# Sums of weight blocks on VectorE in place of accumulating DMAs, in the gate pairs and the heads' projection of a hybrid decoder block

## The chip, the core and the metric

The kernel runs on one core of a Trainium2 chip. A core has TensorE (PE, matmuls, with its weight loads shown as PEld), ScalarE (ACT), VectorE (DVE), GpSimd (POOL) and SyncE (SP), each with a queue of instructions that it takes in order, and 16 DMA engines that all issuing engines share. The metric is the device time of one execution in microseconds (us).

## The reference

One decoder layer in float32 on 512 tokens and a model width of 1024. What matters here is that nearly all of its work is matrix products with weights from HBM:

```python
hn = rmsnorm(x, g_mix[l])
proj = jnp.einsum('bsd,de->bse', hn, w_in[l])
(xa, ba, ca, za, q, k, v, o, zb, ig, fg, ga, gb) = jnp.split(proj, SPLIT_POINTS, axis=-1)
...
hb = mlstm_chunkwise(q, k, v, ig, fg)            # 4 heads, DK 256, DV 512
yb = jax.nn.sigmoid(o) * hb * jax.nn.silu(zb)
yb = jnp.einsum('bsv,vd->bsd', yb, w_b_out[l])   # the heads' projection
merged = jax.nn.sigmoid(ga) * ya + jax.nn.sigmoid(gb) * yb
x = x + jnp.einsum('bsd,de->bse', merged, w_o[l])
```

ga and gb are the gates, 1024 columns each of `w_in`; `ig` and `fg` are eight columns, one input and one forget gate for each head.

## The kernel before

**Products.** Every float32 operand is split into a high part (rounded to the type that the matmul takes, `whi`, by ACT, L152) and a low rest (`wlo`, by DVE, L153); a product is three matmuls, hi x hi, hi x lo, lo x hi (`mm3`, L205 to L207). Weights come in chunks of 512 rows by 512 columns (1 MB, tile `wraw`, a ring of four) by DMA from SP's queue (L135). Each chunk is split in two halves of 256 rows.

**Strassen pairs.** Most of the projections are done with seven block products in place of eight. `pair` lists, for two by two blocks b11, b21, b12, b22 of the weights, the seven right operands in the order of use: b11, b21, b11 + b12, b22, and so on. The sums are made in place: b11 is the first operand, b12 is then added to it and it is the third, b22 is added and it is the fifth, b21 is added and it is the seventh; b22 is also added to b12 for the sixth. So a pair has four sums of two halves each. A sum is made either by an accumulating DMA on POOL's queue (L159), which reads the block from HBM once more and adds it to the tile in SBUF, or by DVE (L157), which adds one tile to another and thus needs both in SBUF. `third` says which engine makes the sum b12 + b22; the other three are DMAs. Each entry of `operands` is (chunk, sums after its split); `last_use` says when a tile of the ring is free, and `load_free` then loads the next chunk.

**Order of the work.** The order on PE, ACT, DVE and POOL is written out by hand (`manual_schedule`); SP's is set by the scheduler. PE's matmuls of a product come in two parts (banks) of 12 matmuls. After each part `step` calls `tick` (L188): it starts the generators of the part before, splits one half of a chunk (`split_half`, L148, followed by its sums), and advances the generators in `active` by one yield. So a yield is one tick later.

**The stages.** First x is normalised and transposed; then the blocks q, k of heads 1 and 0. Beside these run two generators: `gate_rows` (L650 to L699, the logarithm L663, scans of the input and forget gates on DVE, ending with the row of L689, which PE transposes into `ptc` at L694 and L696) and `left` (L609), which makes the sums of hn for all later Strassen products: four DVE sums (L612, L613, L615, L616) and four splits into `hs` (ACT L620, DVE L622 and L625). Then for each head: a pair for v and o, and, around heads 0 and 2, a pair for z of two heads and one for a gate (gb at head 0, ga at head 2; `sink_gate`). After head 1 there is a pair for q, k of heads 2 and 3. While a gate pair runs, `turn` transposes the finished head (copies `yc`, L745) and writes it to HBM (`yt_d`, 1 MB, POOL's queue, L753), and `recut` loads q and k of the next odd head (`qk_raw`, SP's queue, L765) and cuts them in high and low (L212, L213). `yc` and `qk_raw` use the same place in SBUF, so the loads wait for the write. Then come the convolution, its projection, the heads' projection (a Strassen product with two groups of rows, so that its 14 operands are chunks of `w_b_out`; its left operands are `units`, split one by one by `left_high`, L966 to L978, in the generator `left_heads`, from sums in `hsf`, tiles `yhs`), `w_o`, and the gated embedding.

## Time and profile before

| what | value |
|---|---|
| median of 3 runs | 878.53 us (873.56 to 879.10) |
| the profiled execution | 876.83 us, its span 875.1 us |
| PE busy | 851.2 us, 97% |
| DVE, ACT, POOL busy | 612.3, 482.7, 233.5 us |
| accumulating DMAs on `w_in`, `w_b_out` | 122 and 16, 1.4 and 1.6 us to issue each |
| POOL's DMA queue | 78.1 MB, 46.8% of the time of the 16 DMA engines |
| SP's DMA queue | 91.8 MB, 32.0% |

A group or row of the profile names line, engine, operation and output<-input by the names of the program. Times on a timeline are from the start of the span. "Idle before" is how long the engine stood before the instruction, with the one that released it. PE's matmuls overlap: one of 512 columns is shown as 0.39 us long but the next can start before it ends, so the time that a stop costs is read from start to start.

### The profile page before, as it was taken

What the parts mean: (1) busy time and instruction counts of PE and PEld (TensorE: products, weight loads), DVE (VectorE), ACT (ScalarE), POOL (GpSimd) and SP (SyncE); (2) the same over time, 40 slices, a digit from 0 to 9 for tenths busy, and PEclk for the clock granted to TensorE, in tenths of its full rate; (3) what the DMA queues carried; (4) which work ended last, traced back from release to release, by engine and by line L of the source; (5) the groups of instructions that cost most, each with busy time, mean ns of one, the idle gap of its engine ahead of it and who ended that gap; (6) DMA issues with size and microseconds to landing.
All of it is one profiled execution on the core that took longest, in us unless ns stands there. A gap on an engine that the chain in (4) does not pass through costs nothing.

```text
span 875.1 us, 12147 instructions
## 1 busy us (share of the span) xinstructions
PE 851.2 (97%) x4651; PEld 737.8 (84%) x4651; DVE 612.3 (70%) x798; ACT 482.7 (55%) x700; POOL 233.5 (27%) x230
## 2 busy tenths in 40 slices
PE   7999999999999999999899999999999999999996
PEld 6887888877889988888678999999998888788885
DVE  4777657845677667687558678898986777874465
ACT  6557665656666475566576455555553256534342
POOL 4102213312232424222023324234310214130031
PEclk9999999999999999999999999999999999999998
DMA  8847779999995997789999699899998588994002
GB/s 279 276 145 146 142 169 200 230 277 266 232 216 127 255 243 171 158 228 238 272 234 247 116 213 188 196 157 200 181 302 319 107 194 209 265 332 166 1 1 96
DMA packets 105402, 174.92 MB, mean 200 GB/s; under 512 B 6592, under 2 KB 47616, under 8 KB 104064
## 3 DMA queue, kind: packets, MB, share of 16 engines
q0 software_dynamic: 42256, 78.13, 46.8%
q1 hardware_dynamic: 60784, 91.83, 32.0%
q10 hardware_dynamic: 2304, 4.20, 1.4%
q8 instruction: 36, 0.59, 0.3%
q14 instruction: 22, 0.18, 0.1%
HBM read 157.35 MB, written 16.78 MB: 199 GB/s over the span
## 4 chain that ended last, share of the span: by engine, by line
PE 78%; DMA 6%; DVE 3%; ACT 3%; issue 1%; ACTq 0%; SPq 0%; POOL 0%; POOLq 0%; DVEq 0%
PE mm L206 24%; PE mm L207 24%; PE mm L205 24%; DMA wraw<-in_w_in 2%; DMA wraw<-in_w_b_out 2%; ACT whi L152 1%; DVE wlo L153 1%; DMA qk_raw<-qk_d 1%; PE pv L205 1%; PE pv L206 1%; PE pv L207 1%; PE pty L750 1%; PE sc L207 1%; PE sc L206 1%; PE sc L205 1%
## 5 line engine op out<-in xcount | busy, mean ns | idle before, releaser
L153 DVE TENSOR_TENSOR wlo<-wraw,whi 128x1024 fp32r<-128x1024 f32 x240 | 298.2, 1246 | 142.2 <-ACT whi L152 141.1
L152 ACT ACTIVATE whi<-wraw 128x1024 fp32r<-128x1024 f32 x242 | 253.2, 1054 | 115.4 <-PE mm L207 43.7
L159 POOL DMA_DIRECT2D wraw<-in_w_in x122 | 149.2, 1411 | 341.4 <-DVE wlo L153 240.0
L321 ACT ACTIVATE s<-mm 128x512 f32<-128x512 f32 x84 | 50.1, 597 | 96.1 <-PE mm L207 94.2
L205 PE MATMUL mm<-whi,hs 128*128 128x512 f32 x256 | 100.5, 392 | 1.2 <-ACT whi L152 1.2
L206 PE MATMUL mm<-wlo,hs 128*128 128x512 f32 x256 | 100.6, 393 | 0.8 <-DVE wlo L153 0.8
L207 PE MATMUL mm<-whi,hs 128*128 128x512 f32 x256 | 100.3, 392 | 0.0
L205 PE MATMUL mm<-hn_hi,whi 128*128 128x256 f32 (+1 forms) x304 | 93.9, 309 | 0.0
L207 PE MATMUL mm<-hn_hi,wlo 128*128 128x256 f32 (+1 forms) x304 | 93.7, 308 | 0.2 <-POOL wlo L153 0.2
L206 PE MATMUL mm<-hn_lo,whi 128*128 128x256 f32 (+1 forms) x304 | 93.6, 308 | 0.0
L205 PE MATMUL mm<-hs,whi 128*128 128x256 f32 x320 | 90.9, 284 | 0.0
L206 PE MATMUL mm<-hs,whi 128*128 128x256 f32 x320 | 90.5, 283 | 0.0
L207 PE MATMUL mm<-hs,wlo 128*128 128x256 f32 x320 | 90.5, 283 | 0.0
L205 PE MATMUL mm<-whi,hn_hi 128*128 128x512 f32 x192 | 75.6, 394 | 3.2 <-ACT s L321 3.2
L206 PE MATMUL mm<-wlo,hn_hi 128*128 128x512 f32 x192 | 75.2, 392 | 2.1 <-DVE wlo L153 2.1
L207 PE MATMUL mm<-whi,hn_lo 128*128 128x512 f32 x192 | 74.7, 389 | 0.0
L206 PEld LDWEIGHTS mm<-hs,whi 128*128 128x128 f32 x320 | 61.4, 192 | 0.0
L205 PEld LDWEIGHTS mm<-hs,whi 128*128 128x128 f32 x320 | 61.4, 192 | 0.0
L207 PEld LDWEIGHTS mm<-hs,wlo 128*128 128x128 f32 x320 | 61.4, 192 | 0.0
L207 PEld LDWEIGHTS mm<-hn_hi,wlo 128*128 128x128 f32 x304 | 58.5, 192 | 3.3 <-POOL wlo L153 0.6
L206 PEld LDWEIGHTS mm<-hn_lo,whi 128*128 128x128 f32 x304 | 58.4, 192 | 2.5
L205 PEld LDWEIGHTS mm<-hn_hi,whi 128*128 128x128 f32 x304 | 58.4, 192 | 2.5
(278 smaller groups left out, 1657.7 us busy)
## 6 DMA issues: line engine op xcount, KB each, us to landing
wraw<-in_w_in SPq DMA_DIRECT2D x32, 1024.0 KB, 7.2
wraw<-in_w_in POOLq DMA_DIRECT2D x62, 512.0 KB, 8.2
wraw<-in_w_in SPq DMA_DIRECT2D x48, 512.0 KB, 5.3
wraw<-in_w_in POOLq DMA_DIRECT2D x60, 256.0 KB, 5.8
wraw<-in_w_b_out SPq DMA_DIRECT2D x8, 1024.0 KB, 7.0
wraw<-in_w_b_out POOLq DMA_DIRECT2D x16, 512.0 KB, 7.1
yt_d<-yc POOLq DMA_DIRECT2D x4, 1024.0 KB, 7.0
wraw<-in_w_a_out SPq DMA_DIRECT2D x4, 1024.0 KB, 5.4
```

The source lines that it names most:

```text
L152: act.activation(hi, t, AF.Copy)
L153: (e_lo or dve).tensor_tensor(lo, t, hi.bitcast(F32), ALU.subtract)
L159: nc.gpsimd.dma_start(raws[to][:, ks, cs], src[:, ks, :], accum_op=ALU.add)
L205: pe.matmul(ps, lhsT=a[0], rhs=b[0], start=first, stop=False, **kw)
L206: pe.matmul(ps, lhsT=a[0], rhs=b[1], start=False, stop=False, **kw)
L207: pe.matmul(ps, lhsT=a[1], rhs=b[0], start=False, stop=last, **kw)
L321: act.activation(to[i], src, AF.Copy, scale=scale)
L750: pe.transpose(pts[v][:, t * P:(t + 1) * P], y[:, t, v * P:(v + 1) * P], ident)
```

## The change

`pair` gets a number in place of an engine: with `on_dve` 1 the sum b12 + b22 is DVE's, as `third` did; with 2 the sums b11 + b12 and b11 + b22 are DVE's too, and the chunks are loaded in the order b11, b12, b21, b22. Both gate pairs get 2 (the first had none, the second one). In the heads' projection the sum b12 + b22 of both groups becomes DVE's; that of group 1 comes after operand 9 and not 8. Chunk b12 of group 0 (`spare`) is loaded not into the ring but into the place of the two `yhs` tiles, once `left_high` has split the last unit made from them (k == 5); `load_free` does not count it in the ring. `left` starts with a yield and is appended beside `gate_rows`, ahead of the second half of the first q, k block. `recut` waits one yield more between its loads and its first cut. The same sums and products are made as before.

```diff
@@ -81,13 +81,18 @@
         for k0 in halves:
             operands.append((chunk(view, k0, pieces), []))
 
-    def pair(view, p1, p2, third=None):
-
-
-        b11, b21, b12, b22 = (chunk(view, k, p) for p, k in ((p1, 0), (p1, HC), (p2, 0), (p2, HC)))
-        t3 = [(b12, b22, third)]
-        operands.extend([(b11, [(b11, b12, None)]), (b21, [] if third else t3), (b11, [(b11, b22, None)]),
-                         (b22, t3 if third else []), (b11, [(b11, b21, None)]), (b12, []), (b11, [])])
+    def pair(view, p1, p2, on_dve=0):
+
+
+
+        where = ((p1, 0), (p2, 0), (p1, HC), (p2, HC)) if on_dve == 2 else ((p1, 0), (p1, HC), (p2, 0), (p2, HC))
+        b11, b21, b12, b22 = (chunk(view, k, p) for p, k in where)
+        if on_dve == 2:
+            b12, b21 = b21, b12
+        e2, e3 = (dve if on_dve >= n else None for n in (2, 1))
+        t3 = [(b12, b22, e3)]
+        operands.extend([(b11, [(b11, b12, e2)]), (b21, [] if e3 else t3), (b11, [(b11, b22, e2)]),
+                         (b22, t3 if e3 else []), (b11, [(b11, b21, None)]), (b12, []), (b11, [])])
 
 
     chunks.append([(w_ple_v[:, k:k + 1, n * CW:(n + 1) * CW], slice(2 * n + k, 2 * n + k + 1), slice(0, CW))
@@ -100,21 +105,23 @@
         pair(w_in_v, [(V + h * DV, DV)], [(O + h * DV, DV)])
         if h % 2 == 0:
             pair(w_in_v, [(ZB + h * DV, DV)], [(ZB + (h + 1) * DV, DV)])
-            pair(w_in_v, [((GB, GA)[h // 2], CW)], [((GB, GA)[h // 2] + CW, CW)], dve if h else None)
+            pair(w_in_v, [((GB, GA)[h // 2], CW)], [((GB, GA)[h // 2] + CW, CW)], 2)
         elif h == 1:
-            pair(w_in_v, *([(Q + i * DK, DK), (K + i * DK, DK)] for i in (2, 3)), dve)
+            pair(w_in_v, *([(Q + i * DK, DK), (K + i * DK, DK)] for i in (2, 3)), 1)
     for c in range(0, KT * P, 2 * P):
-        pair(w_in_v, *([(o + c, 2 * P) for o in os] for os in ((XA, CA), (BA, ZA))), dve)
+        pair(w_in_v, *([(o + c, 2 * P) for o in os] for os in ((XA, CA), (BA, ZA))), 1)
     for n in range(2):
         block(w_a_v, [(n * CW, CW)])
 
     b11, b21, b22, b12 = ([chunk(w_b_v, (2 * g + r) * HC, [(n * CW, CW)]) for g in range(2)]
                           for r, n in ((0, 0), (1, 0), (1, 1), (0, 1)))
-    adds = {1: [(b11, b12, 1)], 5: [(b11, b22, 1)], 7: [(b12, b22, 0)], 8: [(b11, b21, 0), (b12, b22, 1)], 9: [(b11, b21, 1)]}
-    adds.update({0: [(b11, b12, 0)], 4: [(b11, b22, 0)]})
+    spare = {b12[0]: None}
+    adds = {0: [(b11, b12, 0, None)], 1: [(b11, b12, 1, None)], 4: [(b11, b22, 0, None)], 5: [(b11, b22, 1, None)],
+            7: [(b12, b22, 0, dve)], 8: [(b11, b21, 0, None)], 9: [(b12, b22, 1, dve), (b11, b21, 1, None)]}
     for j, u in enumerate((b11, b21, b11, b22, b11, b12, b11)):
         for g in range(2):
-            operands.append((u[g], [(to[i], c[i], None) for to, c, i in adds.get(2 * j + g, ())]))
+            operands.append((u[g], [(to[i], c[i], e) for to, c, i, e in adds.get(2 * j + g, ())]))
+    place_b12 = b12[0]
     for view in (w_o_v, w_pg_v):
         for n in range(2):
             block(view, [(n * CW, CW)], (HC, 0) if view is w_o_v and n == 0 else (0, HC))
@@ -122,22 +129,27 @@
     last_use = {}
     for i, (r, add) in enumerate(operands):
         last_use[r] = i
-        for to, _, _ in add:
+        for to, c, eng in add:
             last_use[to] = i
+            if eng is not None:
+                last_use[c] = i
     state = {"raw": 0, "split": 0, "use": 0}
     raws, splits, pieces, active, fresh = {}, {}, deque(), [], []
 
     def load_raw(between=None):
         i = state["raw"]
         state["raw"] += 1
-        raws[i] = wraw.tile([P, HC, CW], F32, name=f"wraw{i}", tag="wraw")
+        raws[i] = spare[i] if i in spare else wraw.tile([P, HC, CW], F32, name=f"wraw{i}", tag="wraw")
         for src, ks, cs in chunks[i]:
             nc.sync.dma_start(raws[i][:, ks, cs], src)
             if between:
                 between = between()
 
     def load_free():
-        while state["raw"] < len(chunks) and len(raws) < NRAW:
+        while state["raw"] < len(chunks):
+            i = state["raw"]
+            if (spare[i] is None) if i in spare else (sum(c not in spare for c in raws) >= NRAW):
+                break
             load_raw()
 
     def split_tiles(i, h):
@@ -609,6 +621,7 @@
         a11, a12 = (hnf[:, c * HC:(c + 1) * HC, :H2] for c in range(2))
         a21, a22 = (hnf[:, c * HC:(c + 1) * HC, H2:] for c in range(2))
         hsf = [sp.tile([P, HC, H2], F32, name=f"hsf{i}", tag=f"hsf{i}", align_bytes=256) for i in range(2)]
+        yield
         dve.tensor_tensor(hsf[0], a22, a21, ALU.subtract)
         dve.tensor_tensor(hsf[1], hsf[0], a11, ALU.add)
         yield
@@ -708,6 +721,7 @@
         pe.matmul(psg, lhsT=wg[:, k, :], rhs=hn_hi[:, k, :], start=k == 0, stop=False)
         pe.matmul(psg, lhsT=wg[:, k, :], rhs=hn_lo[:, k, :], start=False, stop=k == KT - 1)
     active.append(gate_rows())
+    active.append(left())
     for m in range(4):
         for kt in range(HC):
             mm3(pss[m], [u[kt][:, m * P:(m + 1) * P] for u in w], [u[:, HC + kt, :] for u in hn],
@@ -722,7 +736,6 @@
             yield
         return sink
 
-    active.append(left())
     qk_0 = []
     block_fm(lambda m, ps: keep_qk(m, ps, qk_0))
     drain()
@@ -763,6 +776,7 @@
         raw = hp.tile([P, 2, 4, S], F32, name="qk_raw", tag="vv", align_bytes=256)[:, 0]
         for m in range(4):
             nc.sync.dma_start(raw[:, m, :], qk_d[h][:, m, :])
+        yield
         yield
         yield
         qk.extend(qk_tile())
@@ -963,7 +977,8 @@
     yf = [wbp.tile([P, 2, HC, H2], F32, name=f"yf{h}") for h in range(NH)]
     for h in (0, 2, 1, 3):
         nc.gpsimd.dma_start(yf[h], yt_d[h])
-    hsf = [wbp.tile([P, HC, H2], F32, name=f"yhs{g}") for g in range(2)]
+    hsf = wbp.tile([P, 2, HC, H2], F32, name="yhs", tag="yhs", align_bytes=256)
+    hsf = [hsf[:, g] for g in range(2)]
     units = {}
 
     def left_high(k):
@@ -1004,6 +1019,9 @@
             low = left_high(k)
             yield
             low()
+            if k == 5:
+                spare[place_b12] = wbp.tile([P, HC, CW], F32, name="wraws", tag="yhs", align_bytes=256)
+                load_free()
             if k == 3:
                 yield
                 dve.tensor_tensor(yf[3][:, 0], yf[2][:, 0], yf[3][:, 0], ALU.subtract)
```

DVE's queue where the z projection of head 0 ends and its gate pair begins: `wlo` of chunk `wraw_1192` is the low half of b11, that of `wraw_1280` (before) or `wraw_1360` (after) of b21, which is the second operand; `c`, `sz` and `gty` belong to z. Before:

```order
L153 TENSOR_TENSOR wlo_1429<-wraw_1192,whi_1428 128x1024
L918 TENSOR_TENSOR c<-sz,c 128x512
L922 TENSOR_TENSOR sz<-sz,mm 128x512
L923 TENSOR_TENSOR gty<-gty,sz 128x512
L153 TENSOR_TENSOR wlo_1454<-wraw_1192,whi_1453 128x1024
L918 TENSOR_TENSOR c<-sz,c 128x512
L922 TENSOR_TENSOR sz<-sz,mm 128x512
L923 TENSOR_TENSOR gty<-gty,sz 128x512
L153 TENSOR_TENSOR wlo_1480<-wraw_1280,whi_1479 128x1024
L900 SCALAR_TENSOR_TENSOR gty<-gty,cols 128x512
L153 TENSOR_TENSOR wlo_1501<-wraw_1280,whi_1500 128x1024
L900 SCALAR_TENSOR_TENSOR gty<-gty,cols 128x512
```

After:

```order
L165 TENSOR_TENSOR wlo_1429<-wraw_1192,whi_1428 128x1024
L169 TENSOR_TENSOR wraw_1192<-wraw_1192,wraw_1280 128x1024
L932 TENSOR_TENSOR c<-sz,c 128x512
L936 TENSOR_TENSOR sz<-sz,mm 128x512
L937 TENSOR_TENSOR gty<-gty,sz 128x512
L165 TENSOR_TENSOR wlo_1454<-wraw_1192,whi_1453 128x1024
L169 TENSOR_TENSOR wraw_1192<-wraw_1192,wraw_1280 128x1024
L932 TENSOR_TENSOR c<-sz,c 128x512
L936 TENSOR_TENSOR sz<-sz,mm 128x512
L937 TENSOR_TENSOR gty<-gty,sz 128x512
L165 TENSOR_TENSOR wlo_1480<-wraw_1360,whi_1479 128x1024
L914 SCALAR_TENSOR_TENSOR gty<-gty,cols 128x512
```

Two sums stand between the low halves of the first operand and those of the second; in the queue behind this, two sums more follow the third operand and two the fourth.

DVE's queue ahead of the transposes into `ptc`; `rows` and `carry` are the scans of the gates, `hs` the low halves of `left`, L689 (now L702) the row that PE needs. Before:

```order
L684 SCALAR_TENSOR_TENSOR rows<-rows 4x128
L682 TENSOR_TENSOR carry<-rows 4x1
L684 SCALAR_TENSOR_TENSOR rows<-rows,carry 4x128
L622 SCALAR_TENSOR_TENSOR hs_116<-hsf_561,hs_115 128x1024
L153 TENSOR_TENSOR wlo_645<-wraw_333,whi_644 128x1024
L682 TENSOR_TENSOR carry<-rows 4x1
L684 SCALAR_TENSOR_TENSOR rows<-rows,carry 4x128
L682 TENSOR_TENSOR carry<-rows 4x1
L684 SCALAR_TENSOR_TENSOR rows<-rows,carry 4x128
L622 SCALAR_TENSOR_TENSOR hs_118<-hnf,hs_117 128x1024
L153 TENSOR_TENSOR wlo_670<-wraw_333,whi_669 128x1024
L689 SCALAR_TENSOR_TENSOR rows<-rows 4x512
```

After:

```order
L635 SCALAR_TENSOR_TENSOR hs_114<-hsf_484,hs_113 128x1024
L697 SCALAR_TENSOR_TENSOR rows<-rows 4x128
L695 TENSOR_TENSOR carry<-rows 4x1
L697 SCALAR_TENSOR_TENSOR rows<-rows,carry 4x128
L638 SCALAR_TENSOR_TENSOR hs_120<-hnf,hs_119 128x1024
L165 TENSOR_TENSOR wlo_650<-wraw_333,whi_649 128x1024
L695 TENSOR_TENSOR carry<-rows 4x1
L697 SCALAR_TENSOR_TENSOR rows<-rows,carry 4x128
L695 TENSOR_TENSOR carry<-rows 4x1
L697 SCALAR_TENSOR_TENSOR rows<-rows,carry 4x128
L165 TENSOR_TENSOR wlo_673<-wraw_333,whi_672 128x1024
L702 SCALAR_TENSOR_TENSOR rows<-rows 4x512
```

The low halves `hs` stand ahead of the scans or between the first of them, and none between the last scan and the row.

DVE's queue in the heads' projection from operand 7 to operand 9: `wraw_6603` (now `wraw_6602`) is b22 of group 1, `wraw_6563` (now `wraw_6562`) that of group 0, `wraws` b12 of group 0, `wraw_6782` b12 of group 1, `l` the left units. Before:

```order
L153 TENSOR_TENSOR wlo_6757<-wraw_6603,whi_6756 128x1024
L978 SCALAR_TENSOR_TENSOR l_6729<-yf_6176,l_6729 128x1024
L213 TENSOR_TENSOR mg_6487<-pth,mg_6486 128x2x256 x2
L153 TENSOR_TENSOR wlo_6779<-wraw_6603,whi_6778 128x1024
L153 TENSOR_TENSOR wlo_6800<-wraw_6162,whi_6799 128x1024
L978 SCALAR_TENSOR_TENSOR l_6785<-yf_6173,l_6785 128x1024
L153 TENSOR_TENSOR wlo_6819<-wraw_6162,whi_6818 128x1024
L153 TENSOR_TENSOR wlo_6839<-wraw_6229,whi_6838 128x1024
L978 SCALAR_TENSOR_TENSOR l_6824<-yf_6175,l_6824 128x1024
L153 TENSOR_TENSOR wlo_6857<-wraw_6229,whi_6856 128x1024
```

After:

```order
L165 TENSOR_TENSOR wlo_6756<-wraw_6602,whi_6755 128x1024
L169 TENSOR_TENSOR wraws<-wraws,wraw_6562 128x1024
L993 SCALAR_TENSOR_TENSOR l_6728<-yf_6176,l_6728 128x1024
L225 TENSOR_TENSOR mg_6486<-pth,mg_6485 128x2x256 x2
L165 TENSOR_TENSOR wlo_6778<-wraw_6602,whi_6777 128x1024
L169 TENSOR_TENSOR wraws<-wraws,wraw_6562 128x1024
L165 TENSOR_TENSOR wlo_6799<-wraw_6162,whi_6798 128x1024
L993 SCALAR_TENSOR_TENSOR l_6784<-yf_6173,l_6784 128x1024
L165 TENSOR_TENSOR wlo_6817<-wraw_6162,whi_6816 128x1024
L165 TENSOR_TENSOR wlo_6836<-wraw_6228,whi_6835 128x1024
L169 TENSOR_TENSOR wraw_6782<-wraw_6782,wraw_6602 128x1024
L993 SCALAR_TENSOR_TENSOR l_6821<-yf_6175,l_6821 128x1024
```

Behind each half of operand 7 stands the sum for group 0, and behind the first half of operand 9 that for group 1, ahead of a left unit.

## Rows read from the trace of the kernel before

**Rows 1.** The page's first part, and one row of the busy time by stage, with columns: the stretch in us from the span's start, its length, busy us (and instruction count) of PE, PEld, DVE, ACT and POOL, the granted TensorE clock (1.00 is full speed), the share of the 16 DMA engines (what overlaps counts twice) and GB/s. The stretch is the fifth product of head 0's gate pair.

```profile
PE 851.2 (97%) x4651; PEld 737.8 (84%) x4651; DVE 612.3 (70%) x798; ACT 482.7 (55%) x700; POOL 233.5 (27%) x230
...
189.00:196.50 7.50, 5.54 (x16) 3.91 (x15) 3.05 (x3) 3.46 (x4) 2.13 (x2) 0.77 1.04 284
```

**Rows 2.** TensorE's timeline where the gate rows are transposed into `ptc`: start, us, engine, line, operation, output<-input, form, count, and in brackets the idle time before it with what ended it. From 73.15 to 76.55 eight matmuls start.

```profile
68.86 0.77 PE L694 MATMUL ptc<-ident,rows 4*128 4x4 f32 x10
71.78 0.41 PE L696 MATMUL ptc<-ident,rows 4*128 4x4 f32 x4 [2.14 <-DVE rows L689]
...
73.15 0.61 PE L206 MATMUL mm<-hn_lo,whi 128*128 128x512 f32 x1
...
76.55 0.41 PE L205 MATMUL mm<-whi,hn_hi 128*128 128x512 f32 x1
```

**Rows 3.** Timeline of VectorE and ScalarE ahead of that (columns as before): the step of the gate rows before the logarithm, the logarithm, a low half of weights, and the row that `ptc` is made of.

```profile
47.21 0.41 DVE L660 TENSOR_SCALAR rows<-rows 4x512 f32<-4x512 f32 x1 [1.36 <-ACT rows L658]
...
52.79 0.63 ACT L663 ACTIVATE rows<-rows 4x512 f32<-4x512 f32 x1
...
66.39 1.23 DVE L153 TENSOR_TENSOR wlo<-wraw,whi 128x1024 fp32r<-128x1024 f32 x1 [2.31 <-ACT whi L152]
...
71.05 0.67 DVE L689 SCALAR_TENSOR_TENSOR rows<-rows 4x512 f32<-4x512 f32 x1
```

**Rows 4.** TensorE's timeline in the gate pair of head 0. From 184.70 to 189.69 there are 22 starts, from 189.69 to 196.07 ten.

```profile
184.70 0.39 PE L206 MATMUL mm<-wlo,hs 128*128 128x512 f32 x1
...
189.69 0.39 PE L207 MATMUL mm<-whi,hs 128*128 128x512 f32 x1
191.29 0.51 PE L205 MATMUL mm<-whi,hs 128*128 128x512 f32 x1 [1.21 <-ACT whi L152]
192.55 0.76 PE L206 MATMUL mm<-wlo,hs 128*128 128x512 f32 x1 [0.76 <-DVE wlo L153]
...
196.07 0.40 PE L205 MATMUL mm<-whi,hs 128*128 128x512 f32 x1
...
204.20 0.50 PE L205 MATMUL mm<-whi,hn_hi 128*128 128x512 f32 x1 [0.45 <-ACT s L321]
...
206.41 0.49 PE L206 MATMUL mm<-wlo,hn_hi 128*128 128x512 f32 x1 [0.31 <-DVE wlo L153]
...
212.90 0.50 PE L206 MATMUL mm<-wlo,hn_hi 128*128 128x512 f32 x1 [0.74 <-DVE wlo L153]
```

**Rows 5.** TensorE's timeline at the end of the gate pair of head 2 and the beginning of the pair after it.

```profile
429.70 0.50 PE L205 MATMUL mm<-whi,hn_hi 128*128 128x512 f32 x1 [2.80 <-ACT s L321]
...
431.91 0.49 PE L206 MATMUL mm<-wlo,hn_hi 128*128 128x512 f32 x1 [0.31 <-DVE wlo L153]
...
438.40 0.50 PE L206 MATMUL mm<-wlo,hn_hi 128*128 128x512 f32 x1 [0.74 <-DVE wlo L153]
```

**Rows 6.** TensorE's timeline in the heads' projection, operand 11.

```profile
756.42 0.50 PE L205 MATMUL mm<-whi,l 128*128 128x512 f32 x1 [0.30 <-ACT whi L152]
757.68 0.50 PE L206 MATMUL mm<-wlo,l 128*128 128x512 f32 x1 [0.76 <-DVE wlo L153]
```

**Rows 7.** DMA issues (output<-input, issuing queue, count, KB each, median us from issue to landing): accumulating DMAs between 150 and 215; a write of `yt_d` at 179 (after head 0), at 406 (head 2) and at 282 (head 1); three loads of `qk_raw` from 417.7; and from the chain of waits (start, us, what) the accumulate that the fifth gate product of head 0 needs.

```profile
wraw<-in_w_in POOLq DMA_DIRECT2D x13, 512.0 KB, 9.5
yt_d<-yc POOLq DMA_DIRECT2D x1, 1024.0 KB, 14.4
yt_d<-yc POOLq DMA_DIRECT2D x1, 1024.0 KB, 8.8
yt_d<-yc POOLq DMA_DIRECT2D x1, 1024.0 KB, 5.2
qk_raw<-qk_d SPq DMA_DIRECT2D x3, 256.0 KB, 9.8
176.86 13.29 DMA wraw<-in_w_in
```

**Rows 8.** The groups of instructions: sums of weights on VectorE (count, then busy us and mean ns, then idle time before).

```profile
L157 DVE TENSOR_TENSOR wraw<-wraw,wraw 128x1024 f32<-128x1024 f32 x12 | 14.6, 1217 | 0.0
```

**Rows 9.** Timeline of VectorE and ScalarE where the z projection of head 2 ends and its gate pair begins; the last row is two low halves in a row.

```profile
388.82 1.22 DVE L153 TENSOR_TENSOR wlo<-wraw,whi 128x1024 fp32r<-128x1024 f32 x1
...
394.94 1.22 DVE L153 TENSOR_TENSOR wlo<-wraw,whi 128x1024 fp32r<-128x1024 f32 x1
...
396.82 1.23 DVE L153 TENSOR_TENSOR wlo<-wraw,whi 128x1024 fp32r<-128x1024 f32 x1
...
397.95 0.60 ACT L321 ACTIVATE s<-mm 128x512 f32<-128x512 f32 x1 [1.17 <-PE mm L207]
...
412.20 2.36 DVE L153 TENSOR_TENSOR wlo<-wraw,whi 128x1024 fp32r<-128x1024 f32 x2 [0.36 <-ACT whi L152]
```

**Rows 10.** ScalarE's timeline at the end of the gate pair of head 2: the second cut of `qk_raw` and two copies `s` that follow, one tick apart.

```profile
427.50 0.63 ACT L212 ACTIVATE qk<-qk_raw 128x512 fp32r<-128x512 f32 x1 [3.41 <-DMA qk_raw<-qk_d]
...
429.05 0.60 ACT L321 ACTIVATE s<-mm 128x512 f32<-128x512 f32 x1 [0.40 <-ACT c L720]
...
432.04 0.60 ACT L321 ACTIVATE s<-mm 128x512 f32<-128x512 f32 x1 [0.40 <-ACT c L720]
```

**Rows 11.** The load of weights that the change moves in the heads' projection (chain of waits: start, us, what), and the DMA issue of the same tensor on SP's queue that took longest to land, at 650.5 (columns as in rows 7).

```profile
733.00 6.04 DMA wraw<-in_w_b_out
...
wraw<-in_w_b_out SPq DMA_DIRECT2D x1, 1024.0 KB, 16.9
```

## The prediction

> **What bounds the kernel now.** I read the page's first part and the busy time by stage first [rows 1]. TensorE (PE) is busy 97% of the span, so nearly all of the chain of waits is matmuls, and only PE's idle and slow time can be won. In the row of a gate pair the DMA engines are full (1.04) while VectorE (DVE) works 3.05 of 7.5 us: transfers are what is short there, and DVE has room. Then I went through PE's timeline and looked for starts that are too far apart. Its even pace is 22 matmuls of 512 columns in 4.99 us, 0.227 us each (the first two of [rows 4]). It is broken in four places in the middle of the program, and I count what each costs:
> - the transposes of the gate rows wait for the row of L689. 2.92 us lie between the starts, ten small transposes need 0.77: 2.15 lost. A little later eight matmuls take 3.40 us, 0.425 each, the pace of the lower of the clock's two levels (1.2 of 2.4 GHz): 3.40 - 8 x 0.227 = 1.58 lost. Together 3.73 [rows 2].
> - gate pair of head 0, fifth product: ten matmuls take 6.38 us, again with slow ones in them (the granted clock was 0.77 from 189.0 to 196.5): 6.38 - 2.27 = 4.11 lost [rows 1, 4].
> - the three stops after it: idle 0.45, 0.31 and 0.74, and a first matmul 0.1 us longer each time: 1.8 [rows 4]. After the gate pair of head 2 the same three stops: 2.80, 0.31, 0.74, with the 0.1 each 4.15 [rows 5].
> - heads' projection: 0.30 and 0.76, in all 1.3 [rows 6].
>
> That is 15.1 us. The rest of PE's idle time is in parts that the change leaves alone. So the profiled run, 876.8 us, could at best become 861.7.
>
> **The change part by part.** *Left sums.* ScalarE (ACT) and DVE run in order. Before, four sums and four splits of `left` stand in the middle of the chain of scans: L689 ran at 71.05 behind a weight split that had waited 2.31 us for ACT, a carry, a low half of `left` (1.19) and another weight split [rows 3]. Now two low halves of `left` come before the first split and none stands between the last scans and the row (the order above); ACT copies for `left` are through before the scans. I replay it: the four sums, 1.2 us each like other sums of that size [rows 8], now stand ahead of L660 and push it from 47.2 to 50.7; but what waits for it is the logarithm on ACT, which came only at 52.8 because ACT itself was not free sooner [rows 3]. The scans then start no later, some 0.8 us sooner, the first weight split at 64.7 in place of 66.4, and L689 at 68.2, done at 68.9. PE asks at 68.86 + 0.77 = 69.6 [rows 2]. I take 3.6 of the 3.73.
>
> *Gate pairs.* 10 accumulating DMAs go (6 for head 0, 4 for head 2). One took 9.5 us to land (median), the one that the fifth product waited for 13.29 [rows 7]. Ten sums on DVE come for them, 1.22 us each, all of the same form as the 12 already there [rows 8]; two in a row start 1.14 us apart (the last of [rows 9]). Their inputs are loaded long before. The wait for the fifth product goes: 4.11 us. The price is where DVE has no slack. With head 2's times: the first operand's lows are at 388.82 and one tick later, the second's at 394.94 and 396.82. Two sums in front shift these by 2.28, to 397.2 and 399.1, done at 398.45 and 400.33. The second product starts when ACT's `s` is released, 397.9 [rows 9]; PE wants the first low one matmul later, 398.1, and the second after seven, 399.45. So PE stops 0.35 us and then 0.53 more: 0.88 for each gate pair, 1.76 in all. Head 0 has the same order and the same distances. Later sums find DVE idle (it waits for ACT there), so by the fourth operand the lag is gone.
>
> *Later cuts of q and k.* Here the chain was: accumulates in the queue ahead of the 1 MB write of `yt_d`, so that it landed after 14.4 and 8.8 us (5.2 after head 1, where none was ahead) [rows 7]; then `qk_raw`, which needs that tile's place; then ACT, stopped 3.41 us at the second cut [rows 10], with the `s` behind it that PE needs. Now no accumulate of the gate pair stands ahead of that write, and the cuts come a tick (2.73 us) later. With 5.2 us the write of head 2 lands near 412.4 and the first load leaves then. The other three follow the next weight chunk, about 415; at the 9.8 us of before [rows 7] they are there at 424.8, and the second cut is due at 426.6. Head 0 has the same 1.8 us in hand. ACT's tick with a cut and a copy is 2.99 us (start to start of two `s`) [rows 10] against PE's 2.73, so ACT falls behind by 0.26 a tick, and more in the two ticks with a `sg`; I get the second half of the next pair's first operand ready just when it is due. I count 0.2 us lost at each. Gain 1.8 + 4.15 - 0.4.
>
> *Heads' projection.* Four accumulates become four sums, and chunk b12 of group 0 gets a place of its own (the free `yhs`), about 8 us earlier. But b22 of group 0 now stays in the ring until operand 7 is summed. So b12 of group 1 is loaded not at 733.0 but two sums later, 735.3. DVE reaches its sum at 739.7 and stands, with a left unit and the low of operand 9 behind it. That load took 6.04 us; the worst of this tensor is 16.9 [rows 11]. From its landing DVE needs 3.5 us for sum, left unit and low; PE wants that low 2 x 24 matmuls before the stop at 756.2, at 745.3. A landing of up to 6.4 us is free, 16.9 would cost 10.5. I am nearest to the first row, since it is the same load, and take 0.3.
> The Trainium skill (DMA: Bandwidth & Descriptors, Anatomy of one DMA) gives 2.0 us plus bytes over 436 GB/s for a DMA from GpSimd. Worked out from it, an estimate, 1 MB lands after 4.4 us; if that held for this load nothing would be lost here and the sum would be 0.3 better, and by it an accumulate of half that size would land in 3.2 us, and removing it would be worth far less. The rows show 6 to 17 us for the one and 9.5 for the other under load, so the measurement decides.
>
> *POOL and SP.* 14 issues of 1.2 us leave POOL's queue; the z and yt writes no longer stand behind them. On SP the first `qk_raw` load now stands ahead of a weight chunk after head 0, as it did after head 2; that chunk belongs to the next pair and is wanted some 20 us later. Nothing counted.
>
> **Sum.** 15.1 - 0.1 (left) - 1.76 (DVE lag) - 0.4 (cuts) - 0.3 (heads) = 12.5 us. 876.8 - 12.5 = 864.3. The median of the runs shown is 878.5, 1.7 above the profiled one; since they differ most likely by the waits on DMA that go, I don't add all of that and say 864.5.
>
> **Rivals.**
> - *The cuts stay late.* If the write of `yt_d` is slow for other traffic, ACT stops again: for it, the full DMA engines [rows 1]; against it, the 5.2 us without accumulates ahead. The three stops come back at both heads, less little: 864.3 + 5.6 = 870. No faster than 1%, nearly.
> - *The gate rows stay late.* The four sums of `left` stand in front of L660. If `Ln` and not ACT's own queue was the limit, L689 gains nothing: 864.3 + 3.6 = 868.
> - *DVE as a new stop in the heads' projection* (ends slower). The load of b12 of group 1 is issued beside the accumulates of operand 8. If it lands only when both have, one after the other at 9.5 us each [rows 7], that is 19 us: DVE stands until 754.3, PE loses 12.6, and the clock falls as it did after the stop at the gate rows, 1.6 more [rows 2]: 864.3 - 0.3 + 14.2 = 878.2. It decides from a landing of 17.6 us on; the worst w_b_out row is 16.9 [rows 11]. For it: the in-order queue, with a left unit and the low behind the sum. Against: the 6.04 of the same load, and four accumulates fewer here.
> - *The DVE lag hides* (a wait on ACT or a DMA ahead of it gives way): 862.5.
>
> **How the numbers follow.** Forecast (862.5 to 866.5) 0.52; cuts late 0.2; gate rows late 0.1; lag hidden 0.1; slower 0.04; other small losses 0.04. A change of 1% is about what can be told from none here; measured from the median shown, faster by over 1% means below 869.7. Forecast, hidden lag, gate rows and a half of the late cuts lie there: 0.74. Within 1%: 0.22. Slower: 0.04. The range, 860 to 871, takes in all but the slower rival and the tails that the spread of the runs (873.6 to 879.1) leaves.
>
> **What would show it.** Right: no idle time of PE before `ptc`; no lower clock between 68 and 77 nor in the fifth gate product; two new stops of 0.3 to 0.5 us at the second product of each gate pair, ended by DVE's low; no wait of the cuts for `qk_raw`; the yt writes landing near 5 us; a DVE wait for b12 of group 1 before the sum of operand 9. Wrong: ACT waiting for `qk_raw`, PE waiting over 1 us anywhere between 70 and 850.

## The result and the profile after

The changed kernel takes 866.2 us (median of 4 runs, 865.25 to 866.90) against 878.1 of the kernel before in the same session: a ratio of 0.9874, 95% interval 0.9838 to 0.9910. The profiled execution took 866.33 us (span 864.5), 10.50 less than the one of before. Forecast were 864.5 for the median and 864.3 for the profiled execution.

Of the page's first part, and of the groups of instructions, the line of the sums on VectorE (count, busy us and mean ns, idle time before). They answer to [rows 1] and [rows 8]:

```profile
PE 847.5 (98%) x4651; PEld 734.8 (85%) x4651; DVE 628.8 (73%) x812; ACT 483.2 (56%) x700; POOL 217.5 (25%) x216
...
L169 DVE TENSOR_TENSOR wraw<-wraw,wraw 128x1024 f32<-128x1024 f32 x24 | 29.3, 1221 | 1.0 <-DMA wraw<-in_w_b_out 0.7
```

Twelve sums became 24 (and two more into the tile of the spare place, a group of its own), at the price of before; POOL has 14 instructions less. The waits of TensorE over the whole program (what waited, for what, us in total, times, the longest):

```profile
PE ptp L499 <- DMA pin<-in_p: 4.6, 2, 3.9
PE mm L218 <- DVE wlo L165: 3.2, 6, 0.8
PE mm L219 <- POOL wlo L165: 0.2, 1, 0.2
```

The first is the beginning of the program, which the change leaves alone. Of the rest six stops for a low half from DVE are left and 0.2 us for one from POOL; the waits for ACT and for the row of the gate rows are gone.

**Where the time came from.** TensorE runs the same matmuls in the same order in both kernels, so each can be paired with itself in the other trace, and the difference of the two starts is what has been won up to there. The difference between two such points is exact to a few hundredths, where a count of idle times misses the slow first matmuls and the clock. Of TensorE's timeline before, three of these points that stand in no group above:

```profile
11.67 0.42 PE L205 MATMUL mm<-whi,pT 128*128 128x512 f32 x1
...
175.42 0.39 PE L205 MATMUL mm<-whi,hn_hi 128*128 128x512 f32 x1
...
406.34 0.39 PE L205 MATMUL mm<-whi,hs 128*128 128x512 f32 x1
```

and TensorE's timeline after, with the same matmuls (11.20, 72.15, 172.29, 188.83, 205.37, 400.10, 429.50, 747.28) and stops between them:

```profile
11.20 0.39 PE L217 MATMUL mm<-whi,pT 128*128 128x512 f32 x1
...
68.99 0.38 PE L709 MATMUL ptc<-ident,rows 4*128 4x4 f32 x4
...
72.15 0.39 PE L217 MATMUL mm<-whi,hn_hi 128*128 128x512 f32 x1
...
162.64 0.50 PE L218 MATMUL mm<-wlo,hn_hi 128*128 128x512 f32 x1 [0.30 <-DVE wlo L165]
...
172.29 0.39 PE L217 MATMUL mm<-whi,hn_hi 128*128 128x512 f32 x1
...
188.83 0.39 PE L217 MATMUL mm<-whi,hs 128*128 128x512 f32 x1
...
205.37 0.50 PE L218 MATMUL mm<-wlo,hn_hi 128*128 128x512 f32 x1 [0.75 <-DVE wlo L165]
...
386.83 0.50 PE L218 MATMUL mm<-wlo,hn_hi 128*128 128x512 f32 x1 [0.31 <-DVE wlo L165]
...
400.10 0.39 PE L217 MATMUL mm<-whi,hs 128*128 128x512 f32 x1
...
429.50 0.50 PE L218 MATMUL mm<-wlo,hn_hi 128*128 128x512 f32 x1 [0.75 <-DVE wlo L165]
...
747.28 0.39 PE L218 MATMUL mm<-wlo,l 128*128 128x512 f32 x1
```

With their partners of before (76.55 in [rows 2]; 196.07 and 212.90 in [rows 4]; 438.40 in [rows 5]; 757.68 in [rows 6]) the gain up to each point and in each stretch is, in us:

| stretch, ends before -> after | gain up to here | in this stretch | forecast |
|---|---|---|---|
| start of the program, 11.67 -> 11.20 | 0.47 | +0.47 | 0 |
| gate rows, 76.55 -> 72.15 | 4.40 | +3.93 | +3.63 |
| first operands of head 0's gate pair, 175.42 -> 172.29 | 3.13 | -1.27 | -0.88 |
| fifth product, 196.07 -> 188.83 | 7.24 | +4.11 | +4.11 |
| cuts after head 0, 212.90 -> 205.37 | 7.53 | +0.29 | +1.6 |
| first operands of head 2's gate pair, 406.34 -> 400.10 | 6.24 | -1.29 | -0.88 |
| cuts after head 2, 438.40 -> 429.50 | 8.90 | +2.66 | +3.95 |
| heads' projection, 757.68 -> 747.28 | 10.40 | +1.50 | +1.0 |

The last 0.1 comes in the last stage. So the one large miss is at the cuts: 2.95 us won of 5.55. ACT's timeline shows that the wait left there is another than the one that the change was to end. It is, after head 0, with the same split after head 2 as the last row:

```profile
191.07 0.60 ACT L333 ACTIVATE s<-mm 128x512 f32<-128x512 f32 x1 [1.17 <-PE mm L219]
193.01 1.06 ACT L164 ACTIVATE whi<-wraw 128x1024 fp32r<-128x1024 f32 x1 [1.34 <-DMA wraw<-in_w_in]
193.97 0.62 ACT L224 ACTIVATE qk<-qk_raw 128x512 fp32r<-128x512 f32 x1
194.50 0.61 ACT L734 ACTIVATE c<-c 128x512 f32<-128x512 f32 x1
195.14 0.33 ACTq L735 DMA_DIRECT2D sg_d<-c  x1
195.51 0.60 ACT L333 ACTIVATE s<-mm 128x512 f32<-128x512 f32 x1 [0.40 <-ACT c L734]
196.51 1.06 ACT L164 ACTIVATE whi<-wraw 128x1024 fp32r<-128x1024 f32 x1 [0.40 <-DMA wraw<-in_w_in]
...
417.64 1.06 ACT L164 ACTIVATE whi<-wraw 128x1024 fp32r<-128x1024 f32 x1 [1.78 <-DMA wraw<-in_w_in]
```

No cut waits for `qk_raw`. What ACT waits for is `wraw`: the split of the seventh operand needs the fourth sum, b11 + b21, the one that is still an accumulating DMA. From there to 206.7 each tick of ACT is 3.0 to 3.5 us long (split, cut, copy `c`, issue of its write, `s` or `sg`), longer than TensorE's 2.73, so the lateness isn't made good. The DMA issues between 170 and 215 (KB each, median us to landing; they answer to [rows 7]):

```profile
wraw<-in_w_in POOLq DMA_DIRECT2D x7, 512.0 KB, 10.7
...
yt_d<-yc POOLq DMA_DIRECT2D x1, 1024.0 KB, 4.7
qk_raw<-qk_d SPq DMA_DIRECT2D x4, 256.0 KB, 3.6
```

The write of `yt_d` now lands after 4.7 us and the loads behind it after 3.6; the accumulates that are left still take 10.7. After head 2 it is 4.8, 9.0 and 10.6.

### The profile page after: what moved, and what is told of

Read it like the earlier page. It is cut to its first block, busy times and chain, and to the rows that moved or that the text cites. A ratio compares the mean times of both kernels' runs of the same rounds, so it can differ in the third digit from the quotient of the medians.

```text
span 864.5 us, 12127 instructions
## 1 busy us (share of the span) xinstructions
PE 847.5 (98%) x4651; PEld 734.8 (85%) x4651; DVE 628.8 (73%) x812; ACT 483.2 (56%) x700; POOL 217.5 (25%) x216
## 4 chain that ended last, share of the span: by engine, by line
PE 83%; issue 6%; DMA 4%; DVE 3%; ACT 2%; POOL 1%; ACTq 0%; POOLq 0%; SPq 0%; DVEq 0%
PE mm L218 25%; PE mm L219 25%; PE mm L217 25%; DMA wraw<-in_w_in 3%; DVE wlo L165 1%; PE pv L217 1%; PE pv L218 1%; PE pv L219 1%; ACT whi L164 1%; DMA z_d<-c 1%; PE sc L219 1%; PE sc L218 1%; PE sc L217 1%; DVE wraw L169 1%; DMA pin<-in_p 0%
## 5 line engine op out<-in xcount | busy, mean ns | idle before, releaser
L171 POOL DMA_DIRECT2D wraw<-in_w_in x112 | 136.9, 1436 | 310.7 <-DVE wlo L165 218.0
```

Of the source, the lines that this page charges most:

```text
L171: nc.gpsimd.dma_start(raws[to][:, ks, cs], src[:, ks, :], accum_op=ALU.add)
```

## The experiments

Ten more kernels ran. The kernel before took 877.6 us (median) beside the first four, 876.6 beside the next four and 877.0 beside the last two. For each run the gains of the stretches are worked out as in the table, against the trace of before. Each comes from one profiled execution and so can hold chance: the start of the program, which no edit touches, differs from that of before by -0.58 (e1) to +1.35 us (e7).

| run | median us | ratio to before, 95% | gate rows | first operands (both) | fifth product | cuts, head 0 / 2 | heads' projection |
|---|---|---|---|---|---|---|---|
| the change | 866.2 | 0.9874, 0.9838 to 0.9910 | +3.93 | -2.56 | +4.11 | +0.29 / +2.66 | +1.50 |
| e1 left sums alone | 874.4 | 0.9965, 0.9949 to 0.9981 | +3.90 | 0 | -0.68 | -1.13 / -0.12 | -0.96 |
| e2 gate pairs alone | 873.3 | 0.9943, 0.9921 to 0.9965 | 0 | -2.56 | +4.12 | +0.82 / +2.83 | +0.36 |
| e3 heads' projection undone | 868.7 | 0.9885, 0.9861 to 0.9908 | +3.90 | -3.19 | +4.10 | +0.70 / +2.84 | -0.38 |
| e4 later cuts undone | 867.4 | 0.9875, 0.9852 to 0.9898 | +3.93 | -2.65 | +4.12 | 0 / +2.59 | +1.51 |
| e5 fourth sum on DVE | 862.3 | 0.9830, 0.9808 to 0.9852 | +3.94 | -2.59 | +4.10 | +2.26 / +4.56 | +1.48 |
| e6 first sum later | 863.4 | 0.9844, 0.9822 to 0.9866 | +3.91 | -0.30 | +4.12 | +0.98 / +2.75 | +0.73 |
| e7 writes of `sg` on POOL | 866.7 | 0.9881, 0.9860 to 0.9902 | +3.53 | -2.51 | +4.09 | -1.75 / +3.81 | +1.40 |
| e8 e5, e6 and e7 together | 862.7 | 0.9834, 0.9812 to 0.9856 | +3.91 | -1.46 | +4.12 | +2.32 / +4.64 | +0.64 |
| e9 e5 and e6 together | 860.9 | 0.9813, 0.9790 to 0.9837 | +3.94 | -0.39 | +4.11 | +2.26 / +4.56 | +1.52 |
| e10 old order of loads | 866.5 | 0.9881, 0.9852 to 0.9911 | +3.92 | -3.81 | +4.12 | +1.25 / +3.08 | +1.51 |

What stands under "first operands" is each time the stretch from the point ahead of that gate pair, so that of head 2 takes in all from 205 us on.

**e1, the left sums alone.** The kernel before with

```diff
+        yield
         dve.tensor_tensor(hsf[0], a22, a21, ALU.subtract)
...
     active.append(gate_rows())
+    active.append(left())
...
-    active.append(left())
```

> The kernel before with nothing but the other moment of the left sums. Theory (the four gains stand apart from each other): the stop ahead of the transposes into ptc (2.15 us) and the slow matmuls behind it (1.58) go, all later stops stay: 3.6 us less than before, about 874.5 against 878.1. Rival (what is won at the gate rows is lost again at a later DMA wait, since the loads of weights come no sooner): 0 to 2 us less. Second rival (the sums ahead of the scans delay the logarithm): no change.

It is 3.1 us faster (0.35% of 877.6; interval 1.7 to 4.5). The gate rows give the 3.9 that they give in the full change. In the profiled execution (876.4 us, above its median) most of it is lost again further on, at waits for DMAs that the full change removes; TensorE's timeline in the gate pair of head 0:

```profile
188.86 0.50 PE L205 MATMUL mm<-whi,hs 128*128 128x512 f32 x1 [1.58 <-ACT whi L152]
```

That is the stop of [rows 4] at 191.29, there 1.21, longer by 0.37; the stop of 0.45 there is 1.60 here. So the term is right. The median (3.1) lies between theory (3.6) and first rival (0 to 2), and its interval reaches to both; that part of an early gain is eaten by transfers that come no sooner is what this one trace shows, and the times alone don't.

**e2, the gate pairs alone.** The kernel before with the new `pair`, and `2` for both gate pairs:

```diff
-            pair(w_in_v, [((GB, GA)[h // 2], CW)], [((GB, GA)[h // 2] + CW, CW)], dve if h else None)
+            pair(w_in_v, [((GB, GA)[h // 2], CW)], [((GB, GA)[h // 2] + CW, CW)], 2)
```

> The kernel before with nothing but the three sums on DVE and the other order of loads in the two gate pairs; left sums, heads' projection and the number of yields ahead of the cuts as before. Theory: the fifth product's wait (4.11 us) goes; the new stops at the first operands are 0.47, 0.47 and 0.31; the stops at the cuts fall from 1.8 + 4.15 to the 3.57 that the trace after shows, because the write of yt_d lands early even without the later cuts: 5.2 us less than before, about 872.9. Rival (the later cuts are needed, ACT waits for qk_raw again and stops as before): 4.11 - 1.25 = 2.9 us less, about 875.2.

It is 5.0 us faster (interval 3.1 to 6.9), as the theory has it: the fifth product gives 4.12, the first operands take 2.56, and the cuts give 3.65 although they come as early as before. The rival's 2.9 lies just outside the interval, and its mark, a wait of ACT for `qk_raw`, is not in the trace.

**e3, the heads' projection undone.** The kernel after with the sums of `w_b_out` as before:

```diff
-    spare = {b12[0]: None}
-    adds = {0: [(b11, b12, 0, None)], 1: [(b11, b12, 1, None)], 4: [(b11, b22, 0, None)], 5: [(b11, b22, 1, None)],
-            7: [(b12, b22, 0, dve)], 8: [(b11, b21, 0, None)], 9: [(b12, b22, 1, dve), (b11, b21, 1, None)]}
+    adds = {1: [(b11, b12, 1, None)], 5: [(b11, b22, 1, None)], 7: [(b12, b22, 0, None)], 8: [(b11, b21, 0, None), (b12, b22, 1, None)], 9: [(b11, b21, 1, None)]}
+    adds.update({0: [(b11, b12, 0, None)], 4: [(b11, b22, 0, None)]})
...
-    place_b12 = b12[0]
+    spare = {}
```

> The kernel after with the heads' projection as before (four sums by accumulating DMAs, b12 of group 0 in the ring). Theory: the two stops in operand 11 (0.30 and 0.76 idle) are back and nothing else: 1.3 us more than after, about 867.5. Rival (those stops came from the timing of the stages ahead and not from the sums): no change against after.

1.0 us more than the change by the ratios, well inside both intervals, so the time alone doesn't settle it; TensorE's timeline does: the stretch loses 1.88 against the change. The two stops of [rows 6] are back, the first longer:

```profile
748.55 0.50 PE L216 MATMUL mm<-whi,l 128*128 128x512 f32 x1 [0.70 <-ACT whi L163]
749.81 0.50 PE L217 MATMUL mm<-wlo,l 128*128 128x512 f32 x1 [0.76 <-DVE wlo L164]
```

**e4, the later cuts undone.** The kernel after with

```diff
-        yield
         yield
         yield
         qk.extend(qk_tile())
```

> The kernel after with the cuts of q and k one tick earlier, as before. Theory A (the loads of qk_raw, issued from 180.7 and 404.9 us on with 3.6 us to land, are there long before either moment; what makes ACT late is its wait for the last accumulate, 1.34 and 0.40 us after head 0, 1.78 after head 2): no change, within 0.5 us of after, no wait of ACT for qk_raw, and PE's four stops of 0.75 or so as after. Theory B (the extra tick is what took the three stops away): ACT waits for qk_raw again, 3 to 5.6 us more than after. Theory C (the number of heavy ticks of ACT counts): up to 1 us less than after.

No change (0.9875 against 0.9874). ACT's first cut after head 0 starts in the tick before, with nothing to wait for, and then ACT waits for the same accumulate:

```profile
190.07 0.62 ACT L224 ACTIVATE qk<-qk_raw 128x512 fp32r<-128x512 f32 x1
...
193.45 1.06 ACT L164 ACTIVATE whi<-wraw 128x1024 fp32r<-128x1024 f32 x1 [1.50 <-DMA wraw<-in_w_in]
```

So Theory A: the extra yield does nothing here. The gain at the cuts comes with the early landing of the write of `yt_d`, which e2 has too without that yield (4.7 and 4.8 us, where it was 14.4 and 8.8). Whether the accumulates ahead in its queue made it late before, or the load that they put on the DMA engines, no run separates.

**e5, the fourth sum on DVE.** The kernel after with

```diff
-                         (b22, t3 if e3 else []), (b11, [(b11, b21, None)]), (b12, []), (b11, [])])
+                         (b22, t3 if e3 else []), (b11, [(b11, b21, e2)]), (b12, []), (b11, [])])
```

> The kernel after with the fourth sum of the two gate pairs, b11 + b21, on DVE as well, so that no accumulating DMA is left in them. Theory A (the four stops at the cuts come from ACT's wait for the last accumulate, 1.34 + 0.40 us after head 0 and 1.78 after head 2, behind which its copies, cuts and splits stand in order): all four stops go, 0.96 + 0.92 + 0.78 + 0.91 = 3.57 us less than after, about 862.6. Theory B (ACT's tick with a cut, a copy and the issue of a write, 3.0 to 3.5 us against 2.73 of PE, is what makes it late): the stops stay, at most 1 us less. Rival (b21 kept longer in the ring delays the weights of the next pair): slower than after, with PE stopped by a load at the next pair's first operands.

862.3 us, 0.44% or 3.9 us below the change by the ratios (their intervals meet only at 0.984 to 0.985); the cuts give 6.82 in place of 2.95, 3.87 more. ACT's timeline at the same place, and of the waits of TensorE over the whole program the one that answers to the 3.2 of the change:

```profile
190.69 0.60 ACT L333 ACTIVATE s<-mm 128x512 f32<-128x512 f32 x1 [1.17 <-PE mm L219]
191.19 1.05 ACT L164 ACTIVATE whi<-wraw 128x1024 fp32r<-128x1024 f32 x1
...
193.68 0.60 ACT L333 ACTIVATE s<-mm 128x512 f32<-128x512 f32 x1 [0.40 <-PE mm L219]
...
196.67 0.60 ACT L333 ACTIVATE s<-mm 128x512 f32<-128x512 f32 x1 [0.40 <-ACT c L734]
```

```profile
PE mm L218 <- DVE wlo L165: 0.6, 2, 0.3
```

The split follows the `s` at once, ACT's ticks are still 3.0 us long (193.68 to 196.67 between two `s`), and all four stops at the cuts are gone. The length of the tick alone stops nobody. The next pair lost nothing by the chunk b21 that stays longer in the ring.

**e6, the first sum behind the second operand.** The kernel after with

```diff
-        operands.extend([(b11, [(b11, b12, e2)]), (b21, [] if e3 else t3), (b11, [(b11, b22, e2)]),
+        t1 = [(b11, b12, e2)]
+        operands.extend([(b11, [] if e2 else t1), (b21, (t1 if e2 else []) if e3 else t3), (b11, [(b11, b22, e2)]),
```

> The kernel after with the first sum of the two gate pairs, b11 + b12, behind the low halves of the second operand and not of the first. Theory (the two sums ahead of the second operand's low halves are what stops PE at 162.6, 386.8 and 392.4): these three stops go, 0.47 + 0.47 + 0.31 = 1.25 us less than after, about 864.9. Rival (the wait moves to the third operand, whose split by ACT needs the sum): no change or slower by up to 1 us.

863.4 us. The first operands lose 0.30 in place of 2.56, so the lag is nearly twice the 1.25 of the theory, which counted idle times of over 0.2 us only; the small stops and slow first matmuls beside them are as much again. DVE's timeline in the change shows the cause, the sum of the first half ahead of the second half of the same operand:

```profile
158.30 1.23 DVE L169 TENSOR_TENSOR wraw<-wraw,wraw 128x1024 f32<-128x1024 f32 x1
...
161.37 1.22 DVE L165 TENSOR_TENSOR wlo<-wraw,whi 128x1024 fp32r<-128x1024 f32 x1
```

TensorE stops for that second row, until 162.64 (above). In the heads' projection this run won 0.73 in place of 1.50, by a stop of 0.45 us for a left unit that e9, with the same edit, does not have.

**e7, the writes of `sg` issued by POOL.** The kernel after with

```diff
-            nc.scalar.dma_start(sg_d[g + n][:, t, :], sg)
+            nc.gpsimd.dma_start(sg_d[g + n][:, t, :], sg)
```

> The kernel after with the sixteen writes of the gates' sigmoids issued from POOL's queue in place of ACT's. ACT's tick falls by 0.40 us for each write, from 3.0 to 2.6 and from 3.5 to 2.7. Theory A (the wait for the last accumulate starts the lateness, and the length of the tick only keeps it): the first stop after the wait stays or is halved (0.96 and 0.78 to 0.9 and 0.4), the second of each goes: about 2.2 us less than after, 864.0. Theory B (the tick is the cause): all four go, 3.6 us less. Rival (the writes now stand behind accumulates on POOL's queue, or cost more there): no change or slower.

No change in time (0.9881), but the trace separates the two causes. ACT's and TensorE's timelines after head 0, and a row of the busy time by stage (columns as in [rows 1]):

```profile
197.54 1.06 ACT L164 ACTIVATE whi<-wraw 128x1024 fp32r<-128x1024 f32 x1 [2.02 <-DMA wraw<-in_w_in]
```

```profile
198.65 0.49 PE L217 MATMUL mm<-whi,hn_hi 128*128 128x512 f32 x1 [1.19 <-ACT whi L164]
199.91 0.80 PE L218 MATMUL mm<-wlo,hn_hi 128*128 128x512 f32 x1 [0.76 <-DVE wlo L165]
```

```profile
200.00:203.50 3.50, 3.50 (x9) 2.78 (x10) 2.88 (x4) 3.16 (x6) 1.38 (x3) 0.54 0.69 176
```

With ACT's tick short, the second stop of each head is gone, and the first is there, as Theory A has it; the 2.2 us that it forecast are not won, and the time is as the rival has it. After head 0 it is worse: the accumulate came later (a wait of 2.02 where it was 0.40), and the clock fell to its lower level (0.54). Its second half was issued at 184.06, in the change at 184.44, but took 13.5 us to land in place of 12.1; the reason was not tested.

**e8, all three edits.**

> The kernel after with the three edits together: fourth sum on DVE, first sum behind the second operand, writes of the sigmoids on POOL's queue. By theory A 3.57 + 1.25 = 4.8 us less than after, about 861.3, with no stop of PE over 0.3 us between 70 and 850. Rival: no better than the best of the three alone, since POOL's queue or the ring of weight tiles gives back the rest.

862.7 us, no better than e5. Two new stops of TensorE, 0.49 us at 235.5 and 0.52 at 457.5, stand where the next pair of each head is summed by accumulates. The time is as the rival has it; what gives the rest back is not shown.

**e9, the fourth sum on DVE and the first one later.** The edits of e5 and e6.

> The kernel after with the fourth sum on DVE and the first sum behind the second operand, the writes of the sigmoids as in after (their move alone changed nothing). Theory A (the two edits act at different places and add up): the three stops at the first operands and the four at the cuts all go, 1.25 + 3.57 = 4.8 us less than after, ratio to before about 0.982, some 1.2 us below the fourth sum alone. Theory B (PE then meets the accumulating DMAs of the next pair, which come no sooner: new stops at 234 to 236 and 456 to 458 as with all three edits, 0.65 and 0.68 us): no better than the fourth sum alone.

860.9 us, the fastest: 16.1 less than before (0.9813), 1.5 below e5 by the ratios. That last step is inside both intervals, but the traces bear it out: the first operands lose 0.39 in place of 2.59. TensorE's waits over the whole program are now these two, so Theory A, and the two stops of e8 are not there.:

```profile
PE ptp L500 <- DMA pin<-in_p: 4.6, 2, 3.7
PE mm L220 <- POOL wlo L166: 0.2, 1, 0.2
```

That the writes on POOL made those two is not shown by it, since e10, with the writes on ACT, has the first of them.

**e10, the old order of loads.** The kernel after with

```diff
-        where = ((p1, 0), (p2, 0), (p1, HC), (p2, HC)) if on_dve == 2 else ((p1, 0), (p1, HC), (p2, 0), (p2, HC))
+        where = ((p1, 0), (p1, HC), (p2, 0), (p2, HC))
...
-        if on_dve == 2:
-            b12, b21 = b21, b12
```

> The kernel after with the chunks of the two gate pairs loaded in the order of before (b11, b21, b12, b22); the same sums on DVE. Now b12 is the third load and no longer the second: it leaves at 150.0 and 374.2 us, and the first sum of b11 + b12 on DVE is due at 158.3 and about 382.4. Theory A (a load lands after 7.5 us, the median here): it is there 0.8 us ahead, no change against after, within 0.6 us. Theory B (the load takes 9 us or more, as accumulates run beside it): DVE stands in front of the sum with the second low half of the same operand behind it, and PE stops for 1 to 3 us in each gate pair: 2 to 6 us slower than after.

No change beyond 0.6 us (0.9881), and DVE waits for no load ahead of the first sum after either head. Theory A: the third load is still in time; the new order is a reserve that isn't drawn on. The -3.81 in the table isn't lost at the first operands: the 1.25 that it is worse than the change are lost between 205 and 402 us, 0.8 of them at a stop of 0.53 us at 237.24, which is at the matmul of e8's stop at 235.5.

## Why the prediction was right, and where its steps were not

The time (866.2 for 864.5, in the range and at the upper edge of the forecast's own band) and the direction were right, and what made them so is above all two terms, each shown apart from the rest of the change: the left sums (e1) and the fifth product (its stretch in e2). Point by point:

- *Left sums*, 3.6 forecast: 3.93 in every run that has the edit but e7, 3.9 alone. The row of L689, now L702, ran 3.15 us earlier than in [rows 3], to 68.57 where the replay had 68.9; the transposes wait no more (68.99 above) and the clock stays up. The row on DVE, and the busy time by stage (columns as in [rows 1]):

```profile
67.90 0.67 DVE L702 SCALAR_TENSOR_TENSOR rows<-rows 4x512 f32<-4x512 f32 x1
```

```profile
73.00:77.00 4.00, 4.00 (x19) 3.30 (x19) 2.78 (x4) 3.86 (x6) 0.00 (x0) 1.00 1.12 203
```

- *Fifth product*, 4.11: exactly that.
- *DVE's lag*, 1.76: 2.56, and e6 gives 2.3 of it back. The mechanism held and the size was short. The step replayed the lows of the second operand and took the first operand's own second half as given. So two stops, at 162.64 and 386.83, are there that the forecast did not have, ahead of those that it had; these stand idle 0.13 and 0.14 us (168.76 and 392.95) and not 0.35 to 0.53.
- *Cuts*, gain 5.95 less 0.4: 2.95. This is the term that was mis-sized, and it hides a step that was missed. "I count 0.2 us lost at each" went from ACT's tick of 2.99 against 2.73 and looked at the waits for `qk_raw` alone. The fourth sum stays an accumulate, and the split that needs it stands on the same in-order queue among the cuts. Before, a wait for `qk_raw` covered it, as ACT's timeline of the kernel before shows (a cut, then the split, with no idle time):

```profile
198.60 0.63 ACT L212 ACTIVATE qk<-qk_raw 128x512 fp32r<-128x512 f32 x1 [2.01 <-DMA qk_raw<-qk_d]
...
199.61 1.05 ACT L152 ACTIVATE whi<-wraw 128x1024 fp32r<-128x1024 f32 x1
```

With that wait gone the accumulate ended last, and the 0.4 became 3.0. e5 removes it and wins 3.87, more than the 3.0 that are missing from 5.95, because 5.95 was itself too small. The forecast priced a stop by its idle time and 0.1 us for the matmul behind it, and left out some 0.16 ahead of it. For the first stop of [rows 5], TensorE's timeline before has the matmul in front:

```profile
426.52 0.39 PE L207 MATMUL mm<-whi,hs 128*128 128x512 f32 x1
```

From there to 429.70 lie 3.18 us, 2.95 more than the even pace of 0.227, where 2.80 were counted, and the 0.1 comes on top. Read like this the six stops cost 6.8 us up to 212.90 and 438.40. So the missed wait cost 3.9, and it is luck that 0.9 of it doesn't show in the time. The accumulate itself was slower than before, too: after head 0 its halves landed after 9.6 and 12.1 us (issued at 183.30 and 184.44, beside the loads of `qk_raw`), where they had taken 8.4 and 9.5 (issued at 188.76 and 192.79). Whether the earlier loads did that, no run shows.
- *The extra yield* was counted as part of that gain: it is worth nothing that the runs can tell (e4). The landing of `yt_d`, forecast at 5.2 us, was 4.7. By the Trainium skill (DMA: Bandwidth & Descriptors, Anatomy of one DMA) the estimate for 1 MB is 4.4 us: near, once no accumulate is queued ahead, while accumulates of half the size still land after 10.7 against its 3.2. The load that the forecast worked its estimate out for, b12 of group 1, left at 726.41 and let DVE go at 731.56, 5.1 us later: between the 4.4 and the 6.04 of [rows 11].
- *Heads' projection*, 1.3 - 0.3: 1.50. DVE stands 0.7 us for b12 of group 1, at the place and for the load that the forecast named, and TensorE doesn't stop for it: the load came within the 6.4 us that the forecast called free. The two stops that went cost 1.5 from start to start up to 757.68, and not 1.3. The row of DVE:

```profile
731.56 1.23 DVE L169 TENSOR_TENSOR wraw<-wraw,wraw 128x1024 f32<-128x1024 f32 x1 [0.68 <-DMA wraw<-in_w_b_out]
```

The rivals: "the cuts stay late" came half true, by another wait than `qk_raw`; "the gate rows stay late", "DVE as a new stop in the heads' projection" and "the lag hides" did not come. The chances that the prediction counts as faster by over 1% add up to 0.82, and not to its 0.74. The misses add up to the 2.0 us between the net gain forecast (12.5) and the one found (10.5): -2.6 at the cuts, -0.8 for the lag, +0.3 and +0.5 at the gate rows and the heads' projection, +0.6 at the start and the end, which no step of the change touches: that much is chance.

## What to carry to other kernels

When a wait is removed, list what else the waiting engine's next instructions wait for, a DMA that landed under the old wait included, and price the second in line; here that was 3.9 us (e5) beside a forecast of 12.5. Work that moves to an engine with room is placed by what is queued behind it in the very next instructions: the same sum one operand later left 0.3 us of a cost of 2.6 (e6). And pair the same matmul in two traces to account for a change, since a list of idle times missed half of the short stops here (it had 1.25 of 2.56 us).

## What the runs showed of the hardware

**The clock after a stop.** Its lower level came after quite different stops, and did not come after others that are as long. Rows of the busy time by stage of the kernel before, after the stops of 2.14 us at the gate rows [rows 2] and of 2.80 after head 2 [rows 5], and of e1 after one of 2.87 at the same place:

```profile
73.00:77.00 4.00, 4.00 (x12) 3.12 (x11) 1.79 (x2) 0.24 (x1) 2.06 (x2) 0.57 1.06 171
...
429.70:433.00 3.30, 2.98 (x12) 2.15 (x13) 2.83 (x4) 2.90 (x5) 0.00 (x0) 1.00 0.61 222
```

```profile
428.20:432.00 3.80, 3.76 (x10) 2.94 (x11) 3.21 (x4) 3.40 (x5) 0.00 (x0) 0.55 0.69 237
```

2.80 and 2.87 us at one place in the program, and the granted clock is 1.00 (2.4 GHz) in the one and 0.55 (1.2 GHz for most of the stretch) in the other. So a stop of this kind has a price of its length or of some 1.5 us more, and what decides it stays open.

**A low half on DVE beside a sum on POOL.** Timeline of DVE and of POOL in the change, after head 0:

```profile
228.85 1.23 DVE L165 TENSOR_TENSOR wlo<-wraw,whi 128x1024 fp32r<-128x1024 f32 x1 [0.97 <-ACT whi L164]
...
230.66 3.06 DVE L165 TENSOR_TENSOR wlo<-wraw,whi 128x1024 fp32r<-128x1024 f32 x1
```

```profile
231.13 1.50 POOL L830 TENSOR_TENSOR pp<-pp 128x384 f32<-128x384 f32 x1
```

The same instruction takes 3.06 us in place of 1.23 where a sum on POOL starts 0.47 us after it, and it does so at 454 us too. Overlap alone doesn't do it: in the kernel before, at the place of that second one, the low half at 463.79 took 1.22 with POOL's sum starting 0.85 us after it. The Trainium skill (SBUF — State Buffer, Who interferes with whom) says that DVE and GpSimd share a pair of ports under an exclusive lock; the two of 3.06 agree with it in direction, though the instruction that got longer is the one that started first, and no run here took the sum away to show the cause.
